# Another order for the seven product forms of a feed-forward stage, and a separate PSUM bank for one of them

## The chip, the cores and the metric

The kernel runs on one core of a Trainium2 chip. The metric is the device time of one execution in microseconds (us), as a median over several executions. Every time below is in us unless it is marked ns. The engines are named as in the profile: PE is TensorE's matmul, PEld its weight load, DVE is VectorE, ACT is ScalarE, POOL is GpSimd and SP is SyncE. SP and POOL here mostly issue DMA transfers: SP the plain loads, POOL the loads that add to what already lies in the buffer.

## What is computed

A trunk of two layers on 256 tokens of width 1024, all float32. Each layer is a feed-forward stage, a mixing stage and a second feed-forward stage. The change touches feed-forward stages only:

```
D_MODEL = 1024; SEQ = 256; DEPTH = 2; D_FF = 2816

def swiglu(h, w_gate_up, w_down):
    a, b = jnp.split(h @ w_gate_up, 2, axis=-1)
    return (jax.nn.silu(a) * b) @ w_down

def hybrid_layer(x, ...):
    x = x + 0.5 * swiglu(rms_norm(x, ffn1_norm), ffn1_w_gate_up, ffn1_w_down)
    ...
    x = x + merged @ w_out
    x = x + 0.5 * swiglu(rms_norm(x, ffn2_norm), ffn2_w_gate_up, ffn2_w_down)
    return x
```

## The kernel before, in words

**Weights in two parts.** The product needs float32 accuracy, and the matmuls work on a narrower form of float32. Each weight tile is therefore split into two parts: `hi` is a rounded copy made by ACT, `lo` is what the rounding left and is made by DVE (`split`, lines 161 and 162). The activations `hx` are split in the same way. A matmul with `hi` covers both parts of the activations (512 columns), one with `lo` covers only the first part (256 columns), so a weight block costs a pair of matmuls.

**Plain units.** The 2816 hidden columns are 22 tiles of 128 columns, and the gate and the up part of one tile form a unit of 1 MB. `unit()` hands out the next unit, and `fetch()` starts the next one: a load into one of four `raw` buffers on SP's queue (line 119), then the split of its two halves. Three units' worth of `hi` and `lo` buffers exist (`parts`, six half-size buffers each), so the split of a unit may begin only when PE has finished the unit three places ahead of it. `pair` runs the 32 matmuls of a unit, and `drain` (ACT line 210, DVE line 211) empties its PSUM tile into `ab`. There are two such PSUM tiles, so a unit can start only when the unit two places ahead of it (among plain units) has been drained. `post` makes silu(a)*b and splits that for the down projection (lines 367 to 370, 233 and 234).

**Seven forms in place of eight products.** In three of the four feed-forward stages (all but the first) the four tiles 12 to 15 are not run as plain units. Their product is cut into 2 by 2 blocks and worked out with seven products of sums, a scheme of Strassen's kind. The tokens' half of each product (the tiles `sf`) is made on chip by `x_forms` (lines 431 to 438). The weights' half is made while loading: a buffer is first written with one block (line 150) and then gets further blocks added by DMA (line 146), with a split between two sums (`sum_form`, splits at lines 156 and 157):

- buffer "a" (`sa`): written for form 1, then added to for forms 5, 6 and 4, in this order
- buffer "b" (`pre`, the space that also holds the normalised activations `xs`): written for form 3, then added to for form 7
- buffer "c": a plain load for form 2 on SP's queue

Written or added, all but form 2 go through POOL's queue. A sum may start only when the split of the form before it in the same buffer has read the buffer, and the first write into `pre` only when `x_forms` has read `xs`. `by_tokens` runs a form: 16 matmuls, half a unit's work. `strassen` then combines the results, which stay in the PSUM banks `pa` (forms 1 and 2), `pe` (5 and 3), `pf` (7 and 4) and `pg` (6).

**The order.** `FEED` is the order of plain units (numbers) and forms (strings) in a stage. The order of the matmuls on PE is that of the code. On ACT, DVE, POOL and SP a scheduler sets the order when the program is built; at run time each engine works through its own list in that order, and an instruction that must wait holds up all that stands behind it on its engine. Two rows of `FORMS` and the functions they feed:

```
FORMS = {
    "1": ("a", False, "11"), "2": ("c", False, "21"), "5": ("a", True, "12"), "3": ("b", False, "22"),
...
        at, add, src = FORMS[f]
...
        if add:
            nc.gpsimd.dma_start(z, w, accum_op=OP.add)
        elif at == "c":
            nc.sync.dma_start(z, w)
        else:
            nc.gpsimd.dma_start(z, w)
```

Of the kernel before, what the change touches and what calls it, by code (L numbers as in the profile page):

```python
# [21 lines left out]
OP = mybir.AluOpType  # L22
# [22 lines left out]
FU = NF + NF // 2 + 24  # L45
LU = FU + NF + NF // 2
GROUP = 12
FEED = (0, 1, 2, 3, 4, 5, "1", 6, "2", 7, "5", 8, "3", 9, 10, "7", 11, 16, "6", 17, 18, "4", 19, 20, 21)
FORMS = {
    "1": ("a", False, "11"), "2": ("c", False, "21"), "5": ("a", True, "12"), "3": ("b", False, "22"),  # L50
    "6": ("a", True, "22"), "7": ("b", True, "12"), "4": ("a", True, "21"),
}


# [4 lines left out]
def trunk_kernel(ctx: ExitStack, tc: tile.TileContext, x_in, w_in, pw_in, qkn_in, rope_in, mask_in, band_in, out):  # L59
# [11 lines left out]
    def quarter(name):  # L71
        return pat.tile([P, 2, S], F32, name=name, tag="at")
# [11 lines left out]
    tt = nc.vector.tensor_tensor  # L84
# [12 lines left out]
    for base in (0, FU, LU, LU + FU):  # L97
        plan.extend([base + n if isinstance(n, int) else (base, n) for n in FEED] if base else range(NF))
        plan.extend(range(base + NF, base + NF + NF // 2))
# [160 lines left out]
    for t in range(PAD - 1):  # L260
        g = min(g for g, w in enumerate(WINDOWS) if t < w - 1)
# [79 lines left out]
    def ffn(after, n0=0, end=False, col=None):  # L341
        gs, gt = {}, {}

        def room(name, n0, m):
            g = acts.tile([P, m, 2, S], F32R, name=name, tag=name)
            gt[name] = g
            gs.update({n0 + i: g[:, i] for i in range(m)})
# [44 lines left out]
        else:  # L392
# [12 lines left out]
            xs = pre[:, :NK * S].rearrange("p (k s) -> p k s", s=S)  # L405
            vt = acts.tile([P, 2, GW], F32, name="vt", tag="v")
            tk = [acts.tile([P, 2, GW], F32, name="tk", tag="tok", bufs=2) for _ in range(2)]
            p1, p5, c12 = tk[0][:, 0], tk[0][:, 1], tk[1][:, 0]
            gq = {tn: vt[:, tn // 2, tn % 2 * S:(tn % 2 + 1) * S] for tn in range(4)}
            sf = {}  # L410

# [31 lines left out]
            def by_tokens(f, ps, first):  # L443

                hi, lo = unit()
                more = {} if first else {"skip_group_check": True}
                for k, (ah, al) in enumerate(sf[f]):
                    wh, wl = blk(hi, 4 * k, 4), blk(lo, 4 * k, 4)
                    prod(ps, ah, wh, first and k == 0, False, **more)
                    prod(ps[:, :S], ah, wl[:, :S], False, False, **more)  # L450
                    prod(ps, al, wh, False, False, **more)
                    prod(ps[:, S:], ah, wl[:, S:], False, k == 3, **more)
                fetch()

            def gated(c, t, n, sign):

                c = c.rearrange("p (i j s) -> p i j s", i=2, j=2)
                sg = small.tile([P, S], F32, name="sg", tag="sg", bufs=2)
                act(by_half(sg), c[:, :, 0, :], AF.Silu, scale=sign)
                stt(by_half(gq[2 * t + n]), c[:, :, 1, :], sign, by_half(sg), op0=OP.mult, op1=OP.mult)  # L460
# [11 lines left out]
            bank = {}  # L472

            def strassen(f):

                b = {"1": "a", "2": "a", "5": "e", "3": "e", "6": "g", "7": "f", "4": "f"}[f]
                fresh = b not in bank
                if fresh:
                    bank[b] = quarter("p" + b).rearrange("p a s -> p (a s)")
                z = bank[b]  # L480
                by_tokens(f, z, fresh)
                if f == "1":
                    act(p1, z, AF.Copy)
                elif f == "2":
                    gated(z, 0, 0, 1.0)
                elif f == "5":
                    act(p5, z, AF.Copy)
                elif f == "6":
                    tt(p1, z, p1, op=OP.add)
                    tt(p5, p5, p1, op=OP.add)  # L490
                    gated(p5, 1, 1, -1.0)
                    tt(c12, bank["e"], p1, op=OP.add)
                    gated(c12, 0, 1, -1.0)
                elif f == "7":
                    tt(p5, z, p5, op=OP.add)
                    room("gb", 16, NF - 16)
                elif f == "4":
                    tt(p1, z, p1, op=OP.add)
                    gated(p1, 1, 0, 1.0)
                    room("gd", 12, 4)  # L500

            late = []
            wait = [0, 1]
            for i, n in enumerate(FEED[2:]):
                if isinstance(n, str):
                    strassen(n)
                    if n == "4":
                        late += [[1, 1], [2, 0]]
                    continue
                pair(unit(), wide(n))  # L510
                fetch()
                if n == 2:
                    scaled_x()
                if n == 3:
                    split_again()
                if n == 4:
                    x_forms()
                for m in wait[:2]:
                    post(m, m < 4)
                wait = wait[2:] + [n]  # L520
                for z in late:
                    z[0] -= 1
                    if z[0] == 0:
                        turned(z[1])
# [3 lines left out]
        for b in range(NK * NF):  # L528
            f, k = divmod(b, NF)
# [125 lines left out]
    def by_half(z):  # L655
        return z.rearrange("p (i c) -> p i c", c=P)
# [230 lines left out]
    for f in range(0, NK, 2):  # L887
        c = L * NG + (f + 2) * S
# [15 lines left out]
    for l in range(L):  # L904
        l_of[0] = l
        ffn(lambda f: prep(f, l, C_GM), len(w3) if l == 0 else 0, col=C_G1)
        if l == 0:
            for d, z in ((rope, rope_in), (mask, mask_in), (qkn, qkn_in)):
                nc.sync.dma_start(d, z)
        mix(l, lambda f: prep(f, l, C_G2))  # L910
        if l + 1 < L:
            ffn(lambda f: prep(f, l + 1, C_G1), col=C_G2)
        else:
            ffn(lambda f: nc.sync.dma_start(out[:, f, :], x[:, f, :]), end=True, col=C_G2)
# [90 lines left out]
```

## Time and profile before

| | |
|---|---|
| median of 3 runs | 1028.94 |
| lowest and highest of them | 1023.43, 1030.81 |
| the profiled execution's own time | 1026.81 |
| its span, first to last instruction | 1025.0 |
| granted TensorE clock, mean | 0.998 |
| DVE busy | 796.3 (78%) |
| ACT busy | 636.8 (62%) |
| POOL busy | 35.0 (3%) |
| DMA traffic | 202.34 MB, 197 GB/s |

The span holds four feed-forward stages and two mixing stages. The three feed-forward stages with forms begin at about 333, 519 and 845; they are called stage A, B and C below. In a row of the timeline the first number is the start and the second the duration, and a note in square brackets gives the idle time of the engine just before the instruction and what ended it. Matmuls are pipelined and their ends are modelled, so that two in a row overlap.

### The profile page before, as it was taken

Reading aid. Unit: us, or ns where it says so; the run is one execution under the profiler, and the core shown is the slowest. Engines: PE = TensorE matmul, PEld = TensorE weight load, DVE = VectorE, ACT = ScalarE, POOL = GpSimd, SP = SyncE. Lnnn points to the kernel's source line nnn. Section 1 sums busy time; section 2 is a strip of 40 time slices with the busy share of each in tenths; the row PEclk is TensorE's granted clock in tenths of the full one; section 3 lists DMA queues with packets and bytes.
Section 4 is the critical chain, followed back from the end, with each engine's and each line's share of the span. In section 5 each row is a group of like instructions: output and inputs, shape, how many; then the busy total and the mean of one; then the engine's idle time right before and its main releaser. Section 6 shows DMA issues by size and latency. Waiting matters only on the chain.

```text
span 1025.0 us, 16029 instructions
## 1 busy us (share of the span) xinstructions
PE 1001.9 (98%) x6324; PEld 903.0 (88%) x6324; DVE 796.3 (78%) x1196; ACT 636.8 (62%) x1011; POOL 35.0 (3%) x64
## 2 busy tenths in 40 slices
PE   9999999999999998899999899999999999989998
PEld 8888889898999887788888788888889998878888
DVE  6998866698887994786689479666988879957852
ACT  7866655567756874575577457556677568745741
POOL 0000000002000010000001000000020000100000
PEclk9999999999999999999999999999999999999999
DMA  8856556554447395565648665565544464956740
GB/s 300 303 200 219 189 206 205 180 184 180 166 152 260 124 269 182 169 242 206 211 159 256 195 205 207 205 205 188 190 171 161 165 247 126 276 179 189 238 164 21
DMA packets 34155, 202.34 MB, mean 197 GB/s; under 512 B 3488, under 2 KB 4768, under 8 KB 13088
## 3 DMA queue, kind: packets, MB, share of 16 engines
q1 hardware_dynamic: 29184, 182.44, 49.9%
q0 software_dynamic: 4896, 18.88, 8.5%
q8 instruction: 49, 0.80, 0.3%
q14 instruction: 26, 0.21, 0.1%
HBM read 200.26 MB, written 1.05 MB: 196 GB/s over the span
## 4 chain that ended last, share of the span: by engine, by line
PE 75%; DVE 11%; DMA 9%; ACT 2%; issue 2%; SPq 0%; ACTq 0%; POOLq 0%
PE ps L89 59%; PE pt L89 6%; DMA pre<-w 5%; PE two L89 4%; DMA sa<-w 3%; DVE lo L162 2%; PE pe L89 2%; DVE lo L157 2%; DVE ab L211 1%; DVE pre L416 1%; PE sc L89 1%; PE pa L89 1%; DVE sg L370 1%; DVE ab L367 1%; DVE hx L422 1%
## 5 line engine op out<-in xcount | busy, mean ns | idle before, releaser
L89 PE MATMUL ps<-hx,hi 128*128 128x512 f32 x1504 | 511.6, 386 | 11.9 <-DVE ab L211 10.3
L162 DVE TENSOR_TENSOR lo<-raw,hi 128x1024 fp32r<-128x1024 f32 (+2 forms) x348 | 411.3, 1190 | 113.8 <-ACT hi L161 112.6
L161 ACT ACTIVATE hi<-raw 128x1024 fp32r<-128x1024 f32 (+2 forms) x348 | 354.2, 1026 | 182.7 <-PE ps L89 126.4
L89 PE MATMUL ps<-hx,lo 128*128 128x256 f32 x1504 | 413.0, 275 | 1.5 <-DVE lo L162 1.5
L89 PEld LDWEIGHTS ps<-hx,hi 128*128 128x128 f32 x1504 | 283.0, 188 | 67.0 <-DVE ab L211 12.4
L89 PEld LDWEIGHTS ps<-hx,lo 128*128 128x128 f32 x1504 | 283.4, 188 | 3.6 <-DVE lo L162 3.6
L89 PE MATMUL ps<-ga,hi 128*128 128x512 f32 (+1 forms) x264 | 87.0, 376 | 0.0
L89 PE MATMUL ps<-ga,lo 128*128 128x256 f32 x256 | 69.9, 273 | 0.0
L89 PE MATMUL ps<-gb,hi 128*128 128x512 f32 (+1 forms) x198 | 65.6, 376 | 0.0
L89 PE MATMUL pt<-hi,hx 128*128 128x512 f32 x192 | 64.9, 384 | 0.0
L89 PEld LDWEIGHTS ps<-ga,hi 128*128 128x128 f32 x264 | 49.0, 188 | 8.3
L89 PE MATMUL pt<-lo,hx 128*128 128x256 f32 x192 | 52.5, 274 | 0.0
L89 PE MATMUL ps<-gb,lo 128*128 128x256 f32 x192 | 52.4, 273 | 0.0
L211 DVE TENSOR_TENSOR ab<-ps,ab 128x512 f32<-128x512 f32 x74 | 50.8, 686 | 0.9
L89 PEld LDWEIGHTS ps<-ga,lo 128*128 128x128 f32 x256 | 48.1, 188 | 0.0
L369 ACT ACTIVATE sg<-ab 128x256 f32<-128x256 f32 x76 | 30.9, 413 | 23.6 <-DVE ab L211 12.8
L89 PE MATMUL ps<-gd,hi 128*128 128x512 f32 (+1 forms) x132 | 44.3, 376 | 0.0
L89 PE MATMUL ps<-gc,hi 128*128 128x512 f32 (+1 forms) x132 | 44.3, 376 | 0.0
L89 PE MATMUL ps<-mk,hi 128*128 128x256 f32 x256 | 44.1, 275 | 0.0
L210 ACT ACTIVATE ab<-ps 128x512 f32<-128x512 f32 x74 | 42.8, 579 | 0.0
L157 DVE TENSOR_TENSOR lo<-sa,hi 128x1024 fp32r<-128x1024 f32 x24 | 29.2, 1218 | 16.8 <-ACT hi L156 16.8
L89 PEld LDWEIGHTS ps<-gb,hi 128*128 128x128 f32 x198 | 36.7, 188 | 6.2
(216 smaller groups left out, 1451.7 us busy)
## 6 DMA issues: line engine op xcount, KB each, us to landing
raw<-w SPq DMA_DIRECT2D x167, 1024.0 KB, 4.9
sa<-w POOLq DMA_DIRECT2D x12, 1024.0 KB, 10.0
pre<-w POOLq DMA_DIRECT2D x6, 1024.0 KB, 12.6
raw<-w SPq DMA_DIRECT2D x16, 256.0 KB, 5.4
out_dram<-gx SPq DMA_DIRECT2D x8, 128.0 KB, 1.9
gx<-x SPq DMA_DIRECT2D x3, 256.0 KB, 5.5
qk<-pw SPq DMA_DIRECT2D x2, 256.0 KB, 2.7
gx<-x SPq DMA_DIRECT2D x1, 300.0 KB, 2.7
```

The lines of the kernel that those rows point to most:

```text
L89: return keep(nc.tensor.matmul(*args, **kw))
L157: tt(lv, a, hv.bitcast(F32), op=OP.subtract)
L161: act(hi, w, AF.Copy)
L162: return tt(lo, w, hi.bitcast(F32), op=OP.subtract)
L210: act(t, ps[:, :, 1, :], AF.Copy)
L211: drained.append(tt(t, ps[:, :, 0, :], t, op=OP.add))
L367: scaled = tt(ab, ab, bc2(r[0]), op=OP.mult) if scale else None
L369: act(sg, ab[:, 0, :], AF.Silu)
L370: tt(sg, sg, ab[:, 1, :], op=OP.mult)
L416: stt(xs[:, k, :], x[:, k, :], c, r[0], op0=OP.mult, op1=OP.mult)
L422: tt(hx[:, k:k + 2, 1, :], xs[:, k:k + 2, :], hx[:, k:k + 2, 0, :].bitcast(F32), op=OP.subtract)
```

## The change

Four things change, all in the stages with forms. `FEED` puts the forms in the order 1, 3, 2, 5, 7, 6, 4 instead of 1, 2, 5, 3, 7, 6, 4, with at least two plain units between two sums into one buffer, and the plain units between them move accordingly. `FORMS` lists them in the same order; what each form loads stays. Form 3 gets a PSUM bank of its own, `ph`, where it had been added on top of form 5's bank `pe`. So the sum of 5 and 3, which PE made before, is made by DVE (`c35`), and form 6 is added to it there: one more addition on DVE in each stage.

```
-FEED = (0, 1, 2, 3, 4, 5, "1", 6, "2", 7, "5", 8, "3", 9, 10, "7", 11, 16, "6", 17, 18, "4", 19, 20, 21)
+FEED = (0, 1, 2, 3, 4, 5, "1", 6, "3", 7, "2", 8, "5", 9, "7", 10, 11, "6", 16, 17, 18, "4", 19, 20, 21)
 FORMS = {
-    "1": ("a", False, "11"), "2": ("c", False, "21"), "5": ("a", True, "12"), "3": ("b", False, "22"),
-    "6": ("a", True, "22"), "7": ("b", True, "12"), "4": ("a", True, "21"),
+    "1": ("a", False, "11"), "3": ("b", False, "22"), "2": ("c", False, "21"), "5": ("a", True, "12"),
+    "7": ("b", True, "12"), "6": ("a", True, "22"), "4": ("a", True, "21"),
 }
...
-            p1, p5, c12 = tk[0][:, 0], tk[0][:, 1], tk[1][:, 0]
+            p1, p5, c35 = tk[0][:, 0], tk[0][:, 1], tk[1][:, 0]
...
-                b = {"1": "a", "2": "a", "5": "e", "3": "e", "6": "g", "7": "f", "4": "f"}[f]
+                b = {"1": "a", "2": "a", "5": "e", "3": "h", "6": "g", "7": "f", "4": "f"}[f]
...
                 elif f == "5":
                     act(p5, z, AF.Copy)
+                    tt(c35, bank["h"], p5, op=OP.add)
                 elif f == "6":
                     tt(p1, z, p1, op=OP.add)
+                    tt(c35, c35, p1, op=OP.add)
+                    gated(c35, 0, 1, -1.0)
                     tt(p5, p5, p1, op=OP.add)
                     gated(p5, 1, 1, -1.0)
-                    tt(c12, bank["e"], p1, op=OP.add)
-                    gated(c12, 0, 1, -1.0)
```

Line numbers behind line 487 rise by one. Two places show how the order of work moves. The first is POOL's queue in stage A; `sa` and `pre` are the buffers "a" and "b", line 150 writes and line 146 adds. Before, the rows are the loads of forms 1, 5, 3, 6, 7 and 4:

```order
L150 DMA sa<-w 128x2x1024
L146 DMA sa<-w 128x2x1024
L150 DMA pre<-w 128x2x1024
L146 DMA sa<-w 128x2x1024
L146 DMA pre<-w 128x2x1024
L146 DMA sa<-w 128x2x1024
```

Now they are those of 1, 5, 3, 7, and then 6 and 4:

```order
L150 DMA sa<-w 128x2x1024
L146 DMA sa<-w 128x2x1024
L150 DMA pre<-w 128x2x1024
L146 DMA pre<-w 128x2x1024
L146 DMA sa<-w 128x2x1024 x2
```

The sum for form 7 has moved ahead of the sum for form 6. The write for form 3 stands where it stood, behind the sum for form 5, although PE now uses form 3 two places before form 5.

The second place is DVE in stage A from the last step of `x_forms` on, with buffer numbers, since rows read alike without them. `raw_3918` is unit 6, `raw_3965` is form 2 and `raw_3996` unit 7; `ps_3852` is the PSUM tile of unit 5. Before:

```order
L434 SCALAR_TENSOR_TENSOR vt_3640<-pre_3638 128x512
L234 TENSOR_TENSOR ga_3530<-sg_3846,ga_3530 128x256
L370 TENSOR_TENSOR sg_3896<-sg_3896,ab_3779 128x256
L162 TENSOR_TENSOR lo_3921<-raw_3918,hi_3919 128x1024
L438 TENSOR_TENSOR sf_3834<-vt_3640,sf_3833 128x512
L211 TENSOR_TENSOR ab_3851<-ps_3852,ab_3851 128x512
L234 TENSOR_TENSOR ga_3530<-sg_3896,ga_3530 128x256
L438 TENSOR_TENSOR sf_3838<-pre_3638,sf_3837 128x512
L162 TENSOR_TENSOR lo_3922<-raw_3918,hi_3920 128x1024
L438 TENSOR_TENSOR sf_3842<-vt_3640,sf_3841 128x512
L157 TENSOR_TENSOR lo_3969<-raw_3965,hi_3967 128x2x2x256
L157 TENSOR_TENSOR lo_3970<-raw_3965,hi_3968 128x2x2x256
```

Now, from the row behind line 434's and its follower on; `ps_3930` is the PSUM tile of unit 6:

```order
L211 TENSOR_TENSOR ab_3851<-ps_3852,ab_3851 128x512
L438 TENSOR_TENSOR sf_3834<-vt_3640,sf_3833 128x512
L370 TENSOR_TENSOR sg_3896<-sg_3896,ab_3779 128x256
L438 TENSOR_TENSOR sf_3838<-pre_3638,sf_3837 128x512
L162 TENSOR_TENSOR lo_3921<-raw_3918,hi_3919 128x1024
L438 TENSOR_TENSOR sf_3842<-vt_3640,sf_3841 128x512
L234 TENSOR_TENSOR ga_3530<-sg_3896,ga_3530 128x256
L162 TENSOR_TENSOR lo_3922<-raw_3918,hi_3920 128x1024
L370 TENSOR_TENSOR sg_3974<-sg_3974,ab_3851 128x256
L157 TENSOR_TENSOR lo_3968<-pre_3638,hi_3966 128x2x2x256
L157 TENSOR_TENSOR lo_3969<-pre_3638,hi_3967 128x2x2x256
L234 TENSOR_TENSOR ga_3530<-sg_3974,ga_3530 128x256
```

The first `lo` of unit 6 has moved behind the drain of unit 5 and two more splits of the tokens' forms, and the split of form 3 from `pre` stands where the split of form 2 stood. Behind these rows come a split of unit 7 (`raw_3996`), the drain of unit 6 and the other split of unit 7.

## The prediction, as put on record before the changed kernel ran

> **What bounds the kernel now.** I read the page's first part, then busy time by stage, PE's timeline in the stages with forms, then POOL's and DVE's timelines there. The page, and the windows of stages A, B and C (stretch, its length, then busy time and instructions of each engine):
>
> ```profile
> PE 1001.9 (98%) x6324; PEld 903.0 (88%) x6324; DVE 796.3 (78%) x1196; ACT 636.8 (62%) x1011; POOL 35.0 (3%) x64
> ...
> 333.00:447.00 114.00, 106.95 (x628) 93.91 (x627) 91.08 (x129) 73.55 (x110) 5.51 (x5) 1.00 0.63 194
> 519.00:631.00 112.00, 107.06 (x620) 93.88 (x619) 90.82 (x129) 72.30 (x109) 5.49 (x5) 0.98 0.65 198
> 845.00:957.00 112.00, 106.62 (x625) 93.55 (x624) 90.62 (x128) 73.16 (x109) 5.50 (x5) 1.00 0.64 196
> ```
>
> PE bounds the kernel: 23.1 of 1025 us are idle, and 7.05 + 4.94 + 5.38 = 17.4 of them lie in these three windows. The change does not touch the number of matmuls, so only idle PE time can be won. PE's timeline says where it lies:
>
> ```profile
> 399.15 0.49 PE L89 MATMUL pf<-hi,sf 128*128 128x512 f32 x1 [1.02 <-ACT hi L156]
> 400.41 0.38 PE L89 MATMUL pf<-lo,sf 128*128 128x256 f32 x1 [0.77 <-DVE lo L157]
> 405.14 0.49 PE L89 MATMUL ps<-hx,hi 128*128 128x512 f32 x1 [2.00 <-DVE ab L211]
> 434.98 0.50 PE L89 MATMUL ps<-hx,hi 128*128 128x512 f32 x1 [2.71 <-DVE ab L211]
> 583.98 0.48 PE L89 MATMUL pf<-hi,sf 128*128 128x512 f32 x1 [1.51 <-ACT hi L156]
> 585.24 0.38 PE L89 MATMUL pf<-lo,sf 128*128 128x256 f32 x1 [0.78 <-DVE lo L157]
> 589.97 0.50 PE L89 MATMUL ps<-hx,hi 128*128 128x512 f32 x1 [1.96 <-DVE ab L211]
> 910.50 0.50 PE L89 MATMUL pf<-hi,sf 128*128 128x512 f32 x1 [0.46 <-ACT hi L156]
> 911.75 0.38 PE L89 MATMUL pf<-lo,sf 128*128 128x256 f32 x1 [0.76 <-DVE lo L157]
> 916.49 0.49 PE L89 MATMUL ps<-hx,hi 128*128 128x512 f32 x1 [1.95 <-DVE ab L211]
> 945.46 0.48 PE L89 MATMUL ps<-hx,hi 128*128 128x512 f32 x1 [1.65 <-DVE ab L211]
> ```
>
> In each stage PE waits for form 7's split (`pf`), and then, one form later, for a drain; in A and C once more, behind form 4. The source is POOL's sums:
>
> ```profile
> 357.23 1.21 POOL L146 DMA_DIRECT2D sa<-w  x1 [52.98 <-DVE lo L157]
> 360.58 0.74 POOL L150 DMA_DIRECT2D pre<-w  x1 [2.15 <-DVE vt L434]
> 374.93 1.19 POOL L146 DMA_DIRECT2D sa<-w  x1 [13.60 <-DVE sg L370]
> 380.74 1.18 POOL L146 DMA_DIRECT2D pre<-w  x1 [4.62 <-ACT tk L487]
> 413.78 1.19 POOL L146 DMA_DIRECT2D sa<-w  x1 [31.86 <-ACT ab L210]
> 545.53 0.73 POOL L150 DMA_DIRECT2D pre<-w  x1 [2.44 <-PE pa L89]
> 565.44 1.18 POOL L146 DMA_DIRECT2D pre<-w  x1 [4.62 <-ACT sg L369]
> 872.46 0.74 POOL L150 DMA_DIRECT2D pre<-w  x1 [2.18 <-DVE vt L434]
> 892.64 1.18 POOL L146 DMA_DIRECT2D pre<-w  x1 [4.61 <-ACT tk L487]
> ```
>
> The times to landing, of `pre` in A, B and C (two transfers each, so the minimum is form 3's write and the maximum form 7's sum) and of `sa` in A (forms 5, 6, 4):
>
> ```profile
> DMA to landing us min/median/max: 7.9/12.5/17.2
> DMA to landing us min/median/max: 8.5/12.9/17.3
> DMA to landing us min/median/max: 8.2/12.4/16.6
> DMA to landing us min/median/max: 8.8/11.9/13.1
> ```
>
> Form 7's sum in A is issued at 380.74, behind form 3's split, and lands at 380.74 + 17.2 = 397.94. ACT and DVE stand still until then:
>
> ```profile
> 398.05 2.00 ACT L156 ACTIVATE hi<-pre 128x1024 fp32r<-128x1024 f32 x2 [12.07 <-DMA pre<-w]
> ...
> 399.13 2.36 DVE L157 TENSOR_TENSOR lo<-pre,hi 128x1024 fp32r<-128x1024 f32 x2 [11.79 <-ACT hi L156]
> ```
>
> The drains of the units before form 7 are queued behind these two on DVE; that is the second wait. Form 4's sum does the same in a smaller way.
>
> **What the removed waits are worth.** The eleven printed waits sum to 6.50 + 4.25 + 4.82 = 15.6. Each costs more than is printed. In an unbroken row a matmul starts before the one ahead has ended:
>
> ```profile
> 365.63 0.39 PE L89 MATMUL ps<-hx,hi 128*128 128x512 f32 x1
> 365.86 0.28 PE L89 MATMUL ps<-hx,lo 128*128 128x256 f32 x1
> ```
>
> Here the second starts 0.16 before the first's end. Behind a wait that overlap is lost, and the matmul itself is 0.10 longer (0.49 for 0.39, 0.38 for 0.28). So 15.6 + 11 x 0.26 = 18.4.
>
> Do they all go? I place the work of A from the end of the new form 3, 373.7 (worked out below), with a form at 2.73 and a unit at 5.49:
>
> ```profile
> 368.13 2.73 PE pa L89 x16
> 370.86 5.49 PE ps L89 x32
> ...
> 552.83 2.75 PE pa L89 x16
> ...
> 880.03 2.73 PE pa L89 x16
> ```
>
> These are rows of the chain of waits: form 2 and unit 7 in A, form 2 in B and in C. Unit 7 then ends at 379.2, form 2 at 381.9, unit 8 at 387.4, form 5 at 390.1, unit 9 at 395.6; form 7 follows, units 10 and 11 reach 409.3, form 6 412.0, units 16 to 18 428.5, then form 4. Form 7's sum is issued when form 3's split is done, at landing 368.5 + 1.2 + 2.3 (from ACT's and DVE's rows above) and an estimated half us for the issue, 372.5 in place of 380.74. Even with the longest landing, 17.3, it is there at 389.8, split by 393.3 (landing + 3.5), 2.3 ahead of PE; the sum for form 6 that shared its flight before is now issued behind it. Form 6's sum needs form 5's split, which in DVE's new order stands eight half splits (1.14 each) and 1.6 of small work behind 372.0: about 383, so it lands by 400 at the worst, against 409.3. Form 4's sum needs form 6's split, whose buffers come free with form 7 at 398.3: about 404, and at 13.1 it lands at 417, against 428.5. No sum is then waited for on PE, and no drain stands behind one for long. I take all 18.4 as gone; if the longest landing returned on form 4's sum, 17.3 would end at 421, still in time.
>
> **What the change adds: form 3 too early for its load.** PE reaches form 3 where it reached form 2 before, at 368.13. But the load of form 3 leaves POOL when it did, since what it waits for (the last step of `x_forms` on line 434, which frees `pre`) has not moved, and the sum for form 5 stays ahead of it. It is issued at 360.58 and lands at 360.58 + 7.9 = 368.5. From landing to the end of the form I take what form 7 shows, end being the next unit's start less its printed wait: A 405.14 - 2.00 - 397.94 = 5.20, B 589.97 - 1.96 - (565.44 + 17.3) = 5.27, C 916.49 - 1.95 - (892.64 + 16.6) = 5.30; mean 5.26. Against the end of form 2 before:
>
> - A: 368.48 + 5.26 - (368.13 + 2.73) = 2.9
> - B: 545.53 + 8.5 + 5.26 - (552.83 + 2.75) = 3.7
> - C: 872.46 + 8.2 + 5.26 - (880.03 + 2.73) = 3.1
>
> together 9.7. Below, this is bounded by a load that comes in time, above by one as slow as form 7's; both are rivals.
>
> Behind the waiting ACT and DVE stand, in DVE's new order, a split of unit 7, the drain of unit 6 and unit 7's other split. The first `lo` of unit 7 is done at landing + 1.2 (start of form 3's `lo`) + 2.3 (both) + 0.3 + 1.2 = 5.0, and PE wants it at 5.3: just in time, with 0.3 to spare. The drain of unit 6 is wanted only by unit 8. DVE's rows for the second and third term:
>
> ```profile
> 360.19 0.42 DVE L234 TENSOR_TENSOR ga<-sg,ga 128x256 fp32r<-128x256 f32 x1
> ...
> 360.87 1.22 DVE L162 TENSOR_TENSOR lo<-raw,hi 128x1024 fp32r<-128x1024 f32 x1
> ...
> 362.00 0.69 DVE L438 TENSOR_TENSOR sf<-vt,sf 128x512 fp32r<-128x512 f32 x1
> 362.60 0.69 DVE L211 TENSOR_TENSOR ab<-ps,ab 128x512 f32<-128x512 f32 x1
> ```
>
> The second edit on DVE is unit 6's first `lo`, at 360.87 before (two rows of 0.34, start to start, behind 360.19). A drain and two splits of `sf` now precede it, 3 x 0.60 from start to start, so it comes 1.8 later and unit 6 ends near 369.3. That is before form 3's `hi` is ready (368.5 + 1.2 = 369.7), so the load covers it: I cost it at nothing, and at 1.2 a stage where the load comes in time. The addition on line 488 is one more DVE instruction of about 0.69 a stage, in a stretch in which DVE stood still for 11.79; nothing on PE waits for it until the work behind form 6. The fifth bank costs nothing either: the pool has four, `pg` now takes the one of `pa`, whose last reader (form 2's gate) is some 20 us earlier.
>
> **The sum.** 18.4 - 9.7 = 8.7 saved. The profiled execution took 1026.8, so it would be 1018.1; it lies 2.1 below the median of 1028.9, on which the same saving gives 1020.2. I predict 1020.
>
> **The rivals.**
>
> *The load comes in time.* Needed is a landing 2.4 before unit 6's end at 369.3, so 6.3 after issue, for `hi` and `lo` of the first half. Then only unit 6's delay stays, 1.2 x 3 = 3.6; the saving is 14.8 and the time 1014. For it: unit 6's own late `lo` holds back the release of a `raw` buffer and with it SP's next load, so the flight is a little emptier. Against: 7.9, 8.5 and 8.2 before, behind the same sum. [...] 12%.
>
> *A second wait behind form 3, as there was behind form 7.* The 0.3 to spare is thin. If unit 7 or the drain behind it waits as the unit behind form 7 did, 2.0 and the 0.26 each, 3 x 2.2 = 6.7 come back and 2.0 is left: 1027. For it: DVE had no gap in this stretch, and now stands still for about 3 us in it. Against: no drain is wanted as early as the one behind form 7. 17%.
>
> *Slower: form 3's load flies as long as form 7's did.* Landing after 17.0 in place of 8.2 makes form 3 end 8.8 later, three times 26.4, and the time 1047. It is slower than before from a landing 8.2 + 8.7 / 3 = 11.1 after issue. For it: form 7's sum also had a sum ahead of it in the queue. Against: this load is a plain write, issued at the same moment behind the same sum as before. 6%.
>
> *The order of the code does not reach the transfers.* If the waits for sums stayed as they were (the queue keeps 5 ahead of 3), only the 9.7 would be new. The queue shows form 7's sum moved ahead of form 6's, so this would need landings of over 20. It would give 1038. 3%.
>
> **Chances.** My forecast has 62%, with its own range 1016 to 1024: 0.8 us of landing up or down in three stages is 2.4, and the runs of before differ by more. The range that takes in the next two rivals is 1013 to 1028. One per cent, about what a measurement of this kernel can tell from no change, is 10.3 us. My 8.7 lies below that; a third of my case and nearly all of the first rival lie above: 0.32 faster. Slower by over 1% are the last two, less what stays within: 0.07. The rest, 0.61, is within 1%.
>
> **What would show it.** After the change, PE's timeline in A, B and C should have a wait at form 3 (`ph`), for ACT's `hi` and DVE's `lo` from `pre`, and none at `pf`, nor 2 us ones for a drain. POOL's sum for form 7 should be issued about 8 us earlier in the stage. Idle PE time in each stage should be about 3. The prediction is wrong if form 3's load lands under 6.3 or over 11 after issue, if unit 7 waits behind it, or if a sum is still waited for at form 7, 6 or 4.

## The result, and the profile after

| | before | after |
|---|---|---|
| median, of 4 runs each | 1027.16 | 1016.13 |
| lowest and highest | 1023.43, 1030.81 | 1015.4, 1016.8 |
| the profiled execution's own time | 1026.81 | 1015.74 |
| its span | 1025.0 | 1014.0 |
| ratio after to before, 95% interval | | 0.9893 (0.9852 to 0.9933) |

The changed kernel is 11.0 us faster, by the medians and by the two profiled executions alike. The forecast was 8.7, to 1020, with 1013 to 1028 as the range.

The first part of the page of after:

```profile
PE 1000.9 (99%) x6324; PEld 906.1 (89%) x6324; DVE 800.2 (79%) x1199; ACT 638.1 (63%) x1011; POOL 35.0 (3%) x64
```

PE's idle time is 1014.0 - 1000.9 = 13.1, where it was 23.1. So 10.0 of the 11.0 are idle time that went. The windows of the stages A, B and C of after (stretch, its length, busy time of PE, PEld, DVE, ACT, POOL, then the granted clock, the DMA engines' share and GB/s):

```profile
333.00:442.00 109.00, 106.85 (x627) 94.98 (x626) 94.26 (x133) 75.63 (x113) 5.51 (x5) 0.98 0.69 212
514.00:624.00 110.00, 106.08 (x621) 94.09 (x621) 94.13 (x133) 74.87 (x112) 5.49 (x5) 0.98 0.68 211
839.00:947.00 108.00, 105.98 (x624) 94.47 (x623) 94.07 (x133) 75.24 (x113) 5.50 (x5) 0.98 0.69 215
```

2.15 + 3.92 + 2.02 = 8.1 idle where the same three had 17.4. The clock of 0.98 in all three is new for A and C, which showed 1.00. PE's timeline of after has these waits in the stages:

```profile
363.74 0.38 PE L89 MATMUL ps<-hx,lo 128*128 128x256 f32 x1 [2.00 <-DVE lo L162]
543.58 0.38 PE L89 MATMUL ps<-hx,lo 128*128 128x256 f32 x1 [2.00 <-DVE lo L162]
550.00 0.48 PE L89 MATMUL ph<-hi,sf 128*128 128x512 f32 x1 [1.04 <-ACT hi L156]
551.26 0.38 PE L89 MATMUL ph<-lo,sf 128*128 128x256 f32 x1 [0.78 <-DVE lo L157]
868.62 0.38 PE L89 MATMUL ps<-hx,lo 128*128 128x256 f32 x1 [1.98 <-DVE lo L162]
```

The waits at `pf` and the long ones for a drain are gone. What is new stands in unit 6, at its first `lo`, in all three stages; at form 3 (`ph`) PE waits in B alone. POOL's timeline in A shows the sums of forms 5, then (behind the write for 3) 7, 6 and 4:

```profile
357.03 1.21 POOL L146 DMA_DIRECT2D sa<-w  x1 [52.98 <-DVE lo L157]
360.38 0.74 POOL L150 DMA_DIRECT2D pre<-w  x1 [2.14 <-DVE vt L434]
372.53 1.19 POOL L146 DMA_DIRECT2D pre<-w  x1 [11.41 <-DVE lo L157]
383.22 1.18 POOL L146 DMA_DIRECT2D sa<-w  x1 [9.49 <-DVE lo L157]
402.69 1.19 POOL L146 DMA_DIRECT2D sa<-w  x1 [18.29 <-DVE gc L234]
```

Form 7's sum leaves at 372.53 (forecast: 372.5), with no other sum in flight ahead of it. The landings of `pre` in A, B and C (the minimum is form 3's write, the maximum form 7's sum):

```profile
DMA to landing us min/median/max: 8.4/9.9/11.4
DMA to landing us min/median/max: 8.4/9.1/9.9
DMA to landing us min/median/max: 8.0/9.2/10.5
```

Form 7's sum takes 9.9 to 11.4, where it took 16.6 to 17.3. Form 3's write takes what it took.

**Removed and added, measured.** The chain of waits of after has the ends of form 3 in A, B and C as the starts of the piece behind it:

```profile
371.14 2.73 PE ph L89 x15
373.87 5.40 PE ps L89 x32
...
551.26 4.30 PE ph L89 x15
555.55 1.64 PE ps L89 x9
...
868.62 7.11 PE ps L89 x31
875.72 2.67 PE ph L89 x16
878.39 1.70 PE ps L89 x10
```

Unit 6 started at 361.53, 546.25 and 873.43 before and starts at 361.35, 541.19 and 866.25 after, so after is ahead by 0.18, 5.06 and 7.18 there. Form 2, in whose place form 3 now stands, ended at 370.86, 555.58 and 882.75 before. The added part is the difference of the ends plus the lead that was lost:

- A: 373.87 - 370.86 + 0.18 = 3.2
- B: 555.55 - 555.58 + 5.06 = 5.0
- C: 878.39 - 882.75 + 7.18 = 2.8

together 11.0. The lead grows by 4.88 in A, 2.12 in B and (up to the 11.0 at the end) 3.82 in C. So what was removed is 4.88 + 3.2 = 8.1, 2.12 + 5.0 = 7.1 and 3.82 + 2.8 = 6.6, together 21.8. The change won twice what the time shows, and gave half of it back at unit 6 and form 3.

**Where B's end of form 3 comes from.** In A and C form 3 ended 5.1 behind the landing of its load (373.87 - 368.75, and 878.39 - 865.26 - 8.0), in B 6.7. The windows of after around unit 6 in A show why such a stretch can be long:

```profile
363.00:364.00 1.00, 0.26 (x2) 0.27 (x3) 1.00 (x2) 0.00 (x0) 0.00 (x0) 1.00 1.03 205
364.00:365.00 1.00, 1.00 (x6) 0.86 (x6) 1.00 (x3) 0.00 (x0) 0.00 (x0) 0.70 1.07 234
365.00:366.00 1.00, 1.00 (x5) 0.81 (x4) 1.00 (x2) 0.00 (x0) 0.00 (x0) 0.50 0.91 360
366.00:367.00 1.00, 1.00 (x5) 0.90 (x4) 0.09 (x1) 0.00 (x0) 0.00 (x0) 0.50 1.02 422
367.00:368.00 1.00, 1.00 (x5) 0.82 (x5) 0.00 (x0) 0.00 (x0) 0.00 (x0) 0.59 1.03 389
368.00:369.00 1.00, 1.00 (x8) 0.88 (x8) 0.00 (x0) 0.23 (x1) 0.00 (x0) 1.00 1.05 426
```

Behind the wait of 2.00 the granted clock is 0.50 for about 3.4 us, and PE runs at about half its pace: a pair takes 0.64 from start to start (364.86 to 365.50), where it is 0.34 at a clock of 1.00 (the counts in brackets take in matmuls that reach into a row from outside it). In C it is the same stretch, behind the wait of 1.98. In B the wait of 2.00 in unit 6 is followed by no such stretch (the clock is 1.00 from 543.60 to 547.40), but the two waits of 1.04 and 0.78 at form 3 are, so it falls into form 3 itself, as PE's timeline shows:

```profile
551.47 0.39 PE L89 MATMUL ph<-hi,sf 128*128 128x512 f32 x1
...
551.81 0.38 PE L89 MATMUL ph<-hi,sf 128*128 128x512 f32 x1
...
552.79 0.63 PE L89 MATMUL ph<-hi,sf 128*128 128x512 f32 x1
...
553.43 0.63 PE L89 MATMUL ph<-hi,sf 128*128 128x512 f32 x1
```

A pair takes 0.64 from start to start instead of 0.34, so 3.3 us at this pace lose about 1.6 (an estimate). That is B's surplus, 6.7 - 5.1.

### The profile page after: what moved, and what is told of

Same layout as the page of the kernel before. It is cut to its first block, busy times and chain, and to the rows that moved or that the text cites. A ratio compares the mean times of both kernels' runs of the same rounds, so it can differ in the third digit from the quotient of the medians.

```text
span 1014.0 us, 16050 instructions
## 1 busy us (share of the span) xinstructions
PE 1000.9 (99%) x6324; PEld 906.1 (89%) x6324; DVE 800.2 (79%) x1199; ACT 638.1 (63%) x1011; POOL 35.0 (3%) x64
## 4 chain that ended last, share of the span: by engine, by line
PE 90%; DVE 6%; DMA 2%; ACT 1%; issue 0%; SPq 0%; ACTq 0%
PE ps L89 70%; PE pt L89 7%; PE two L89 4%; PE pe L89 2%; DMA pre<-w 2%; PE pf L89 2%; DVE lo L162 1%; PE ph L89 1%; PE pa L89 1%; DVE pre L416 1%; PE sc L89 1%; PE pg L89 1%; DVE lo L157 1%; DVE ab L211 1%; DVE ab L367 1%; DVE hx L422 1%
## 5 line engine op out<-in xcount | busy, mean ns | idle before, releaser
L161 ACT ACTIVATE hi<-raw 128x1024 fp32r<-128x1024 f32 (+2 forms) x348 | 354.4, 1028 | 208.9 <-PE ps L89 152.7
L369 ACT ACTIVATE sg<-ab 128x256 f32<-128x256 f32 x76 | 30.7, 410 | 21.3 <-DVE ab L367 10.2
L89 PEld LDWEIGHTS pt<-hi,hx 128*128 128x128 f32 x192 | 36.0, 188 | 6.8
```

Source lines behind the costliest of these rows:

```text
L89: return keep(nc.tensor.matmul(*args, **kw))
L161: act(hi, w, AF.Copy)
L369: act(sg, ab[:, 0, :], AF.Silu)
```

## The experiments

Two questions were open. What removed the waits: the earlier issue and the extra plain units, as the prediction argued, the bank, or the place of form 7's sum in POOL's queue? And what cost the 11.0: the load of form 3, unit 6's late `lo`, or the halved clock behind it? The kernel of before ran on the same chip beside each group of runs. Its medians were 1027.02 (beside e1, e2, e3, e6), 1028.81 (beside e4, e5, e7) and 1025.49 (beside e8). All ratios are to before.

### The bank alone (e1_bank)

The order of before; only form 3 gets its own bank and DVE the sum:

```
-                b = {"1": "a", "2": "a", "5": "e", "3": "e", "6": "g", "7": "f", "4": "f"}[f]
+                b = {"1": "a", "2": "a", "5": "e", "3": "h", "6": "g", "7": "f", "4": "f"}[f]
...
+                elif f == "3":
+                    tt(c35, z, p5, op=OP.add)
                 elif f == "6":
                     tt(p1, z, p1, op=OP.add)
+                    tt(c35, c35, p1, op=OP.add)
+                    gated(c35, 0, 1, -1.0)
...
-                tt(c12, bank["e"], p1, op=OP.add)
-                gated(c12, 0, 1, -1.0)
```

> The order of before with form 3 in a PSUM bank of its own and the additions on DVE as after the change. Theory S (the sums): the gain comes from DMA sums that now land before PE wants them, so the bank alone changes nothing: within 1 us of before (1027), the waits at forms 7 and 4 as before. Theory B (the bank): before, form 3 was added onto form 5's bank and had to wait for its copy, so the bank alone brings most of the 11 us: about 1018.

Measured: 1029.15, ratio 1.0028 (1.0011 to 1.0045). PE's timeline in C still has the waits at form 7 and behind it:

```profile
909.45 0.49 PE L89 MATMUL pf<-hi,sf 128*128 128x512 f32 x1 [1.09 <-ACT hi L156]
...
916.04 0.49 PE L89 MATMUL ps<-hx,hi 128*128 128x512 f32 x1 [1.86 <-DVE ab L211]
```

The wait behind form 4, which the expectation left in place, is down to 0.27 in A and gone in C. PE's idle time falls with it, from 23.1 to 17.7 (1024.4 - 1006.7). But PE's busy time rises from 1001.9 to 1006.7: the granted clock now falls to 0.50 behind the wait for the drain (1.85 to 1.87) in all three stages, where the trace of before has one such stretch. On balance the bank and DVE's sum bring none of the gain; alone they cost 1 to 5 us.

### More plain units before forms 7, 6 and 4, in the order of before (e6_later7)

```
-FEED = (0, 1, 2, 3, 4, 5, "1", 6, "2", 7, "5", 8, "3", 9, 10, "7", 11, 16, "6", 17, 18, "4", 19, 20, 21)
+FEED = (0, 1, 2, 3, 4, 5, "1", 6, "2", 7, "5", 8, "3", 9, 10, 11, "7", 16, 17, "6", 18, 19, "4", 20, 21)
```

> The kernel of before with forms 7, 6 and 4 one plain unit later each and nothing else changed (no new bank, form 3 where it was). Theory S: the wait at form 7 and the wait for a drain behind it (about 4 to 4.5 us in each stage) go, since 7's sum gets 5.5 us more; the one behind form 4 stays or shrinks: 1027 - 12 to 14 = about 1014, with no wait at unit 6 beyond those of before. Rival: the wait is for the place in the queue behind form 6's sum, or moves to form 4: 1020 or more.

Measured: 1027.06, ratio 0.9988 (0.9969 to 1.0008): no gain, where about 1014 was expected. POOL's queue is that of before (form 6's sum at 374.95, form 7's at 380.76), and the landing is as late:

```profile
DMA to landing us min/median/max: 8.4/12.9/17.3
```

PE now has a unit more to do, and indeed does not wait at `pf` in A. It waits in that unit instead, for a drain:

```profile
402.63 0.49 PE L89 MATMUL ps<-hx,hi 128*128 128x512 f32 x1 [4.48 <-DVE ab L211]
```

With 3.11 in B and 4.41 in C these waits sum to 12.0, where the eleven of before have 15.6, so the units did win something. It is lost again to the clock, which falls to half in or behind each of the three, for 17 us in all, where the trace of before has 3.4. The window in B:

```profile
584.30:591.10 6.80, 5.69 (x17) 4.84 (x18) 5.21 (x8) 3.36 (x7) 0.00 (x0) 0.50 0.05 7
```

Two of the eleven runs, with a mean clock of 0.996 and 0.997, took 1021.24 and 1018.55; the others have 0.990 to 0.993. DVE's timeline in A shows where the drain was:

```profile
389.55 0.42 DVE L370 TENSOR_TENSOR sg<-sg,ab 128x256 f32<-128x256 f32 x1
399.28 1.23 DVE L157 TENSOR_TENSOR lo<-pre,hi 128x1024 fp32r<-128x1024 f32 x1 [9.32 <-ACT hi L156]
...
400.76 1.22 DVE L157 TENSOR_TENSOR lo<-pre,hi 128x1024 fp32r<-128x1024 f32 x1
401.90 0.68 DVE L211 TENSOR_TENSOR ab<-ps,ab 128x512 f32<-128x512 f32 x1
```

DVE is ready for form 7's split at 390 and stands still until 399.28; the drain that PE needs is queued behind it. The sum is due when ACT and DVE reach its split in their lists, not when PE reaches the form. A unit more in front of the form puts off only the second.

### Only the place in POOL's queue (e8_hold6)

The order of before on PE, ACT and DVE, and its banks. POOL alone is made to issue form 6's sum behind form 7's (`behind` is the kernel's helper that fixes an order):

```
         if add:
-            nc.gpsimd.dma_start(z, w, accum_op=OP.add)
+            d = nc.gpsimd.dma_start(z, w, accum_op=OP.add)
+            if f == "7":
+                sums_at["7"] = d
+            if f == "6":
+                behind(d, sums_at["7"])
```

> The kernel of before, order of forms, units and banks untouched, with one thing held: POOL issues form 6's sum only behind form 7's, so that its queue reads 1, 5, 3, 7, 6, 4. The order on the other engines is that of before. Theory Q (the place in the queue): form 7's sum is issued at about 380.7 in A as before, but flies without form 6's and lands after about 11 us in place of 17, at 392; ACT and DVE reach it at 387, so the drains are held 5 us in place of 11 and PE waits neither at form 7 nor behind it. About 14 of the 18 us go, the wait behind form 4 stays: 1013 to 1015. Rival (form 7 needs the earlier issue that the exchange of 3 and 5 gives): waits of 1 to 2 us a stage remain, 1018 to 1022.

Measured: 1008.67, ratio 0.9828 (0.9795 to 0.9861), so 1025.49 x 0.0172 = 17.6 faster, where the change brought 11.0 (the two intervals just overlap) and 1013 to 1015 was expected. No wait over 0.4 is left on PE in the stages. POOL's timeline in A (its lines are 4 higher from 150 on):

```profile
356.87 1.21 POOL L146 DMA_DIRECT2D sa<-w  x1 [52.98 <-DVE lo L161]
360.23 0.74 POOL L154 DMA_DIRECT2D pre<-w  x1 [2.15 <-DVE vt L438]
380.40 1.19 POOL L146 DMA_DIRECT2D pre<-w  x1 [19.44 <-ACT tk L491]
381.14 1.67 POOL L146 DMA_DIRECT2D sa<-w  x1
405.71 1.19 POOL L146 DMA_DIRECT2D sa<-w  x1 [22.90 <-DVE lo L161]
```

Form 7's sum is issued when it was, 380.40 for 380.74, and form 6's 6 us later than before. The landings of `pre` in A:

```profile
DMA to landing us min/median/max: 8.1/8.8/9.5
```

9.5 in place of 17.2, at the same issue time. PE, ACT and DVE run the same instructions in the same order as before, so the place in the queue is the whole of the cause: form 6's sum had been ahead, and form 7's had to fly with it or behind it. Form 4's wait, which the expectation left in place, went as well: its sum is issued at 405.71 instead of 413.78, though nothing was done to it. Part of the 17.6 is the clock, which no longer falls behind the waits: its mean was 1.000 in all six runs, and 0.992 to 0.998 in those of before beside them. At 0.995, 0.005 x 1025 = 5 us of PE's pace are lost (an estimate).

### The change with forms 3 and 2 exchanged (e2_swap23)

```
-FEED = (0, 1, 2, 3, 4, 5, "1", 6, "3", 7, "2", 8, "5", 9, "7", 10, 11, "6", 16, 17, 18, "4", 19, 20, 21)
+FEED = (0, 1, 2, 3, 4, 5, "1", 6, "2", 7, "3", 8, "5", 9, "7", 10, 11, "6", 16, 17, 18, "4", 19, 20, 21)
```

> The changed kernel with forms 2 and 3 exchanged: 1, 2, 3, 5, 7, 6, 4. DVE's order up to form 2 is then that of before, with unit 6's first lo early. Theory S: the sums for 7, 6 and 4 still land in time, and form 3 is used one unit and one form (8.2 us) later, so its load lands well before it. The three stages lose their 11 us at unit 6 and form 3 and keep only the short waits of before at unit 6: 1016 - 9.5 = about 1006.5, no half-speed clock in the three stages. Rival: form 7's sum, now issued only behind form 3's later split (about 6 us before landing it would have to share the queue with form 6's), is late again: waits of 2 to 4 us at form 7 in each stage, 1012 to 1018.

Measured: 1008.71, ratio 0.9824 (0.9805 to 0.9843); the expectation was 1006.5. With form 3 a unit and a form later, and unit 6's first `lo` early again on DVE, neither the load nor that `lo` holds up PE as before. In unit 6 waits of 0.2 to 0.33 are left, in unit 7 of B one of 0.86, and there is no stretch at half clock (the mean is 1.000 in all four runs). Of the 11.0 that the change gave back, (0.9893 - 0.9824) x 1027 = 7 are had again by this exchange.

### Form 3's write on another queue (e3_sp)

The changed kernel with form 3's write issued on SP's queue, away from the sum for form 5 on POOL's:

```
-        elif at == "c":
+        elif at in "bc":
             nc.sync.dma_start(z, w)
```

> The changed kernel with the first write of buffer b (form 3's load) issued on SP's queue in place of POOL's, so that it does not stand behind form 5's sum in a queue. DVE's order around unit 6 stays. Theory L (the late load sets the end of form 3, as predicted): the load lands 5 us after issue, form 3 ends 1.5 to 2.5 us earlier in each stage, in all 5 to 7 us: about 1010. Theory U (unit 6 sets it: its late lo makes PE wait 2.0 us, and the clock then falls to half for 3.4 us): stages A and C, which show no wait at form 3, gain under 0.5 us each, and only stage B gains 2 to 3.5: about 1013.

Measured: 1014.78, ratio 0.9885 (0.9863 to 0.9906), that of the change. The write took 8.4, 7.8 and 8.1 to its landing, not 5 (the plain loads on SP's queue have a median of 4.9 in after): the expectation missed, and the run does not tell the late load from unit 6's split, as it was meant to. It does show that the queue is not what makes the write slow. While form 5's sum flies, the DMA engines' share is 1.03 at 205 GB/s (first window row above, of after), and beside it the write takes 8.0 to 8.4 from POOL's queue and 7.8 to 8.4 from SP's.

### The hole in unit 6 filled with matmuls (e4_fill9, e5_fill2)

e3_sp, with 9 or 2 extra matmuls of 512 columns between form 1 and unit 6, whose results are overwritten:

```
                 if f == "1":
                     act(p1, z, AF.Copy)
+                    bank["h"] = quarter("ph").rearrange("p a s -> p (a s)")
+                    for _ in range(9):
+                        prod(bank["h"], one_r, hk[0], True, True)
```

> e3_sp (form 3's load on SP's queue, so that unit 6 alone sets the start of form 3) with nine extra 512-column matmuls on PE between form 1 and unit 6, into form 3's bank before that form starts it; nothing reads them. They run while unit 6's first lo is late and fill the 2.0 us hole. [...] Rival (the half speed comes from something else that happens then, such as the DMA traffic or the split work): the half-speed rows stay and the time is that of e3_sp or a little more.

> As e4_fill9 with two extra matmuls in place of nine: the hole at unit 6 shrinks from 2.0 to about 1.5 us, but PE's work behind it starts no earlier. [...]

Both were expected at 1011.5, which is 1014.8 less about 3 for the slow stretches in A and C; that these would go was the author's estimate. Measured: 1015.22 with 9, ratio 0.9883 (0.9861 to 0.9905), and 1013.29 with 2, ratio 0.9854 (0.9836 to 0.9872). The window of unit 6 in A with 9:

```profile
364.00:367.00 3.00, 3.00 (x19) 2.72 (x19) 2.36 (x4) 0.00 (x0) 0.00 (x0) 1.00 1.01 322
```

The half clock is gone: 1.00 in this window. But PE then waits for form 3, as its timeline shows:

```profile
369.64 0.49 PE L89 MATMUL ph<-hi,sf 128*128 128x512 f32 x1 [0.24 <-ACT hi L156]
370.90 0.38 PE L89 MATMUL ph<-lo,sf 128*128 128x256 f32 x1 [0.77 <-DVE lo L157]
```

With 2 the hole shrinks to 1.55 in all three stages, and in this execution the clock stays at 1.00:

```profile
363.73 0.38 PE L89 MATMUL ps<-hx,lo 128*128 128x256 f32 x1 [1.55 <-DVE lo L162]
370.62 0.38 PE L89 MATMUL ph<-lo,sf 128*128 128x256 f32 x1 [0.77 <-DVE lo L157]
```

So a full-speed unit 6 only runs into the late load. The delayed `lo` with its slow stretch, and the load, each hold form 3 until about the same time; taking away one of them wins at most 1.5 us of the 11.0 (1013.29 against 1014.78). e3_sp says the same by itself: its run with a mean clock of 1.000 took 1015.38, and the two with 0.997 took 1013.92 and 1015.30. Both kernels missed 1011.5 for that reason.

### The order of before with only forms 3 and 5 exchanged (e7_swap35)

The `FORMS` and banks of the change, with this `FEED`:

```
-FEED = (0, 1, 2, 3, 4, 5, "1", 6, "2", 7, "5", 8, "3", 9, 10, "7", 11, 16, "6", 17, 18, "4", 19, 20, 21)
+FEED = (0, 1, 2, 3, 4, 5, "1", 6, "2", 7, "3", 8, "5", 9, 10, "7", 11, 16, "6", 17, 18, "4", 19, 20, 21)
```

> The order of before with only forms 3 and 5 exchanged (1, 2, 3, 5, 7, 6, 4; form 3 in its own bank, which this order needs); plain units and form 7 stand where they stood before. The POOL queue then has form 7's sum ahead of form 6's, issued about 375 in A in place of 380.7. Theory Q (what made form 7 late was its sum's place behind form 6's in the queue, since e6_later7 showed that more units alone only move the wait to a drain): form 7's sum lands by 388, both waits behind it go, and the time is that of e2_swap23, 1008 to 1010, unless form 4's sum, which has two plain units here, is late (then up to 1013). Rival (the moved plain units are what counts): the waits at form 7 stay, 1018 or more.

Measured: 1006.95, ratio 0.9793 (0.9775 to 0.9811), so 1028.81 x 0.0207 = 21.3 faster, and the lowest ratio of all; 1008 to 1010 was expected. The exchange makes form 6's sum wait for the split of form 5, which now comes after form 3's, and so it falls behind form 7's, as POOL's timeline in A shows:

```profile
375.89 1.19 POOL L146 DMA_DIRECT2D pre<-w  x1 [14.97 <-DVE sg L370]
381.70 1.18 POOL L146 DMA_DIRECT2D sa<-w  x1 [4.62 <-issue]
404.85 1.19 POOL L146 DMA_DIRECT2D sa<-w  x1 [21.97 <-DVE lo L157]
```

Nothing of what the change moved further is needed for the gain.

## Why the prediction came out as it did, point by point

**What is lost before, and where.** Right. All eleven waits that it listed went with the change, and 17.4 - 8.1 = 9.3 of the 11.0 are idle time of PE in A, B and C.

**Why they go.** The outcome was right, and the reason given is shown only in part. The prediction argued that form 7's sum is issued 8 us earlier and has more units in front of it, so that "Even with the longest landing, 17.3, it is there". In A the sum landed at 383.98 instead of 397.94: 8.2 of these 14.0 us come from the earlier issue, 5.8 from a shorter flight (11.4 for 17.2), on which the argument did not count. The earlier issue was not needed: e8_hold6, with the issue where it was and form 6's sum behind it, removed the waits and brought 17.6. More units alone were not enough (e6_later7). So what sufficed is what the prediction mentions only beside its argument: "the sum for form 6 that shared its flight before is now issued behind it". Whether the earlier issue alone would have been enough, behind form 6's sum and with a landing of 17.3, no run shows.

That form 4's sum "does the same in a smaller way" held for the near cause. But e8_hold6 shows that its lateness came with form 7's, and in e1_bank that wait nearly went while those at form 7 stayed, so it hung on little.

**The size of what goes.** 21.8 against 18.4. About 1.6 of it is a stretch at half clock that before has in B behind its wait of 1.96, and that went with the wait. The window of before there:

```profile
591.00:594.00 3.00, 3.00 (x11) 2.58 (x10) 2.20 (x5) 2.59 (x5) 0.00 (x0) 0.51 0.74 309
```

The prediction priced a wait at its length and 0.26. The other 1.8 was not assigned to a cause. That the total was off by only 2.3 is in part luck: 3.4 too little in this term met 1.3 too little in the next.

**Form 3 too early for its load.** The place and the size were right: 11.0 against 9.7. The landings (8.4, 8.4, 8.0 against 7.9, 8.5, 8.2) and the 5.26 from landing to the end of the form (5.1 in A and C) held. The miss is B, 5.0 against 3.7, whose form 3 ran at half clock. (The forecast's 3.1 for C is 3.16 by its own terms, which changes nothing.)

**Unit 6's first `lo`.** Its delay came as forecast, 2.00 against 0.22 in A, which is the 1.8. "I cost it at nothing" then failed as a picture: in A and C the clock fell to half behind the wait, unit 6 ended about 370.7 in A instead of 369.3, and PE showed its wait there and none at `ph` in A and C, where the prediction looked for one. In the time it is a small error, at most 1.5, since the load held the form as long.

**What was costed at nothing.** Unit 7 did not wait, with 0.3 to spare as worked out. In A its first `lo` began at 372.48 and took 1.22, so it was done at 373.70, and PE's first matmul with it began at 373.94. The bank and the sum on DVE brought no gain and by e1_bank cost a little, 1 to 5 us in the order of before.

**The rivals.** None came. The load did not come in time: it landed 8.0 to 8.4 after its issue, where 6.3 was needed, and in e3_sp a write on SP's queue took as long, 7.8 to 8.4. A second wait behind form 3 did not come, nor a landing over 11 for form 3's write. The order did reach the transfers.

**The chances.** 11.0 is 1.07%, just beyond the 10.3 that parted faster from no change; the forecast had that side at 0.32, and the interval of the ratio holds both sides.

## What to carry to other kernels

Where several transfers that add into buffers share a queue, put them in the order in which the engines that read them reach that work in their own lists; the one that is needed first must not stand behind another (form 7's sum in A took 17.2 behind form 6's in before, and 9.5 ahead of it in e8_hold6). More work in front of the consumer on the bounding engine gained nothing here (a ratio of 0.9988 in e6_later7), since DVE between them, which works through its list in order, stood still for 9.32 at the missing data and kept back the drain behind it. And when a step is moved forward, look first at what its load waits for: here the exchange of forms 3 and 5 in `FEED` made the gain (21.3 in e7_swap35), and the changed kernel, with form 3 further ahead still, kept 11.0.

## What the hardware showed that was not expected

**A wait of 2 us can cost 1.6 more.** Waits on PE of 2.00 and 1.98 (A and C of after) and of 1.96 (B of before) were followed by a granted clock of 0.50 for about 3.4 us, and so were the two of 1.04 and 0.78 in B of after and those of 1.85 to 1.87 in e1_bank. Those of 1.55 were not in the trace of e5_fill2. But not each long wait does it: those of 2.00 and 2.71 in A of before (the clock is 1.00 from 405.2 to 409 and from 435 to 439) and of 2.00 in B of after and of e3_sp were not followed by a slow stretch. So the length of a wait alone does not tell whether the clock falls behind it, and what does was not shown: no run was made to find it.

**Sums behind one another.** A transfer of 1 MB that adds (form 7's) took 9.5 to 12.7 in the runs that had nothing of its kind shortly ahead of it (after, e3_sp, e7_swap35, e8_hold6), and 16.6 to 17.3 where one had been issued 6 us earlier (before, and A of e6_later7). While form 5's sum flew in A of after, the DMA engines' share was 1.03 at 205 GB/s; a few us later, behind its landing, it was 1.02 at 422. e8_hold6 shows how two sums go. Form 6's was issued 0.74 behind form 7's, and of the sums of `sa` in A it is the maximum:

```profile
DMA to landing us min/median/max: 8.9/10.5/18.9
```

It landed 10 us behind form 7's (381.14 + 18.9 against 380.40 + 9.5), and form 7's was no slower for it: 9.5 is the shortest of the range above. So of these two sums, issued 0.74 apart, the first took no longer than one alone and the second landed 10 us later.
